# A two-layer trunk on one core: loads and squares at the start, fill ahead of two attention steps, one unit's sums and the last row block

## The chip, the cores and the metric

The kernel runs on one core of a Trainium2 chip. The time is device microseconds of one execution, and less is better. The profile's engines are PE (TensorE), DVE (VectorE), ACT (ScalarE), POOL (GpSimd) and SP (SyncE, which here issues nearly all DMAs).

## What is computed

Sixteen learned rows (meta) are put ahead of 512 input rows of width 1024. Then come one layer of gated linear attention (GLA) and one of differential softmax attention, each an RMSNorm, one wide input projection, the mixing, a gate and an output projection that is added to the rows. A last RMSNorm drops the meta rows.

```python
h = concatenate([meta, x])                       # 528 rows of 1024
for i in range(2):
    hn = rmsnorm(h, g_norm[i])                   # h * rsqrt(mean(h*h) + eps) * g
    y = gla_branch(hn, ...) if i == 0 else diff_branch(hn, ...)
    h = h + y
return rmsnorm(h[16:], g_final)

# diff_branch: q, k, v, z = split(hn @ w_in); per head (8 heads, two maps of width 128):
#   s = q @ k.T / sqrt(128) + bias;  p = softmax(s);  a = p[0] - lam * p[1];  o = a @ v
#   o = o * rsqrt(mean(o*o) + eps) * gnorm * (1 - lambda_init)
#   y = (silu(z) * o) @ w_out
```

## The kernel before

**Arithmetic.** Every f32 operand of a large matmul is held as a high and a low part. ACT copies the high part (line 284), DVE subtracts it to get the low part (line 285), and PE multiplies in three passes. Plain projections run at line 430 with 512 columns. Most others are a `Unit`: a 2x2 block product made of seven smaller ones with 256 or 264 columns (line 440), whose weight sums DVE forms (`sums`, line 375). ACT copies a partial product of a unit out of its bank (`u`, line 461) before PE may add the next product on top of it, and DVE adds the outputs (lines 495 and 497).

**Order of the work.** PE's order is written by hand. Projections are generators in a queue, and a planner `W` deals them out: `W.fill(c)` issues products of about c microseconds of its own estimate and then the next attention step comes. If the queue is empty, a fill issues nothing. A head has 14 steps over four row blocks, taken from block 3 down to block 0: A is the scores and the exponentials, B transposes the softmax rows and splits them (`aT`, `am`), C multiplies by the values (lines 409 and 1773) and normalizes a row block, E transposes two finished blocks (line 1789), multiplies by the gate into `yt` and splits it into `hT`. The last three steps of a head are B(0), C(0) and E(0). C's chain is: ACT puts a constant beside the values (line 1777), squares and sums them (1778), POOL takes the power (1780), ACT scales (1781); line 1789 reads the result `on`. In the last head only the first six steps (A(3), A(2), B(3), A(1), C(3), B(2)) lie between units; the others alternate with the output projection by row block (`final_rows`, called F3 to F0 in that order, each in two parts; line 1863), whose weights ACT and DVE split into tiles called `x`. The orders on DVE, ACT and POOL are the scheduler's, from the program and its own costs, except at the start and in the last row block, where they follow the program text. Every engine takes its instructions in order. `W.mark` is the DVE addition that was issued last; `tc.issue_after(W.mark.ins)` keeps an instruction behind it in the order.

**Start.** SP loads the identity, meta, x in four blocks of 128 rows (`x0` to `x3`: tiles `qs`, `ks`, and the two called `v`), the norm weights, a small weight `glr` and then the large weights (`raw`). For each block ACT squares and sums the rows (line 712), DVE and POOL make the factor (lines 564 and 565), DVE scales the rows in two halves (line 722), and PE transposes them (line 742), four blocks to a bank; unscaled rows are transposed too (730). When the fourth block is in, ACT and DVE take the transposed, scaled rows out of the banks (lines 800 and 801), split them, and the first projection starts. PE runs matmuls of ones (line 656) while it has nothing else.

**End.** F0 adds the last row block's output projection to the rows in three column parts of 512, 256 and 256 (line 1857, DVE), ACT squares and sums each part (1858), DVE adds the three sums (1870, 1871), DVE forms the first half times the last norm's weights, `hg` (1872), POOL takes the power (1873), ACT scales `hg` (1882) while DVE scales the other half (1880), and each half goes out by a DMA (1883).

Of the kernel before, what the change touches and what calls it, by code (L numbers as in the profile page):

```python
# [217 lines left out]
def trunk(ctx, tc, x, meta, g_norm, gla_w_in, gla_w_gate_up, gla_b_gate, gla_gnorm, gla_w_out,  # L218
# [146 lines left out]
    def want_unit(w, c0, calm=False):  # L365
# [11 lines left out]
        def sums(raw):  # L377
            t = T(wp, [P, 2, 512], F32, "sum", bufs=1)
            add(in_rows(t[:, 1, :]), block(raw, 2), block(raw, 3))
# [282 lines left out]
    sp.dma_start(ident, c_ident)  # L662
    xt = []
    grows = T(gp, [16, P], F32, "vm0")
    z2 = T(gp, [P, 2, D], F32, "z")
    v2 = [T(gp, [P, 2, D], F32, f"v{i}") for i in range(2)]
    for b in range(5):
        t0, n = BLK[b]
        t = T(gp, [P, D], F32, ("qs", "ks")[b - 1]) if b in (1, 2) else {0: z2, 3: v2[0], 4: v2[1]}[b][:, 1, :]
        sp.dma_start(t[:n], meta if b == 0 else x[(b - 1) * P:b * P])  # L670
        xt.append(t)
        if b == 2:
            sp.dma_start(grows, g_norm.rearrange("l (k p) -> (l k) p", p=P))
# [32 lines left out]
    sums0 = T(gp, [P, 10], F32, "sums0")  # L706
    raws = {}

    def squares(b):
        sq = z2[:, 0, :]  # L710
        n = BLK[b][1]
        act.activation(sq[:n], xt[b][:n], AF.Square, accum_out=sums0[:n, b:b + 1])

    def factor(b):
        n = BLK[b][1]
        rstd_of(sums0[:n, 5 + b:6 + b], sums0[:n, b:b + 1], D, n)

    def scaled(b, halves=range(2)):
        n = BLK[b][1]
        for i in halves:  # L720
            o = yt[i][:, b - 1, :512] if b else xm0[:NM, i * 512:(i + 1) * 512]
            dve.tensor_scalar(o, xt[b][:n, i * 512:(i + 1) * 512], sums0[:n, 5 + b:6 + b], None, op0=ALU.mult)
# [31 lines left out]
    for k in range(KT):  # L754
        pe.transpose(pm[:, k, :], xm0[:NM, k * P:(k + 1) * P], ident[:NM, :NM])
    raw_copy(1, 0, dve)
# [10 lines left out]
    pe.transpose(pm0[:, KT * NM:KT * NM + 16], grows, ident[:16, :16])  # L767
    turned(2, range(4))
    warm_up(3)
    scaled(3)  # L770
    turned(3, range(4))
    squares(4)
    factor(4)
# [3 lines left out]
    dve.tensor_tensor(xm, pm, g_sb[:, 0, :].unsqueeze(2).to_broadcast([P, KT, NM]), op=ALU.mult)  # L777
    for c in (0, 32, 64):
        act.activation(glr[:, :, c:c + RANK], glr_raw, AF.Copy)
    dve.tensor_tensor(glr[:, :, 96:], glr_raw, glr[:, :, :RANK].bitcast(F32), op=ALU.subtract)  # L780
    raw_copy(2, 0, act)
    raw_copy(2, 1, act)
    warm_up(3)
    scaled(4)
# [18 lines left out]
    scaled_pair(0)  # L803
    for k0 in range(0, KT, 2):
# [1039 lines left out]
    def final_rows(b, wt, yp):  # L1844
# [10 lines left out]
        def finish(i, cs):  # L1855
            hc = hacc[:, b, cs]
            dve.tensor_tensor(hc, hc, ps[i], op=ALU.add)
            act.activation(o[:, cs], hc, AF.Square, scale=1.0 if b else float(D) ** -0.5, accum_out=st[:, i:i + 1])
# [167 lines left out]
```

## Time and profile before

| | |
|---|---|
| median of three runs | 969.67 us (969.65, 969.67, 970.43) |
| profiled execution, its own time | 971.08 us |
| its span on the core | 968.4 us |
| mean granted clock of PE | 0.996 |
| busy: PE, DVE, ACT, POOL | 953.0, 798.2, 635.6, 81.3 us |
| moved by DMA | 104.96 MB, 108 GB/s over the span |

The timeline's rows give the start in microseconds from the span's start, the duration, engine, line, operation, output and inputs, and in brackets how long the engine sat idle before it and what released it. A row with "xN" joins N instructions. The rows of the waits give total, number and longest wait of one line for another. In the table by stage, a row gives the busy time of each engine in a stretch, with the number of instructions, then the granted clock of PE, the busy share of the DMA engines, and GB/s.

### The profile page before, as it was taken

The page shows a single profiled execution, that of the slowest core. Times are in us where ns is not written, and L with a number is a line of the kernel's source. Part 1 is how long each engine was busy: PE and PEld are TensorE (multiplying, and loading weights), DVE is VectorE, ACT ScalarE, POOL GpSimd, SP SyncE. Part 2 cuts the span into 40 slices and gives each one's busy share as a digit, 9 for nine tenths or more (in the row PEclk, how much of TensorE's full clock was granted, in tenths as well). Part 3 has the DMA queues.
Part 4 walks back from the last instruction along what each step waited for, and adds up shares of the span by engine and source line. Part 5 has one row for each costly group of instructions (what it writes and reads, how often), then busy time and mean ns, then how long its engine had stood idle before and what let it go on. Part 6 is the DMA issues. An engine that isn't in the chain of part 4 may idle for free.

```text
span 968.4 us, 18488 instructions
## 1 busy us (share of the span) xinstructions
PE 953.0 (98%) x7173; PEld 912.4 (94%) x7173; DVE 798.2 (82%) x1557; ACT 635.6 (66%) x1313; POOL 81.3 (8%) x164
## 2 busy tenths in 40 slices
PE   9999999999999999999999999999999999999997
PEld 8999999999999999998899898999999999989986
DVE  7989886886878787667997887879879889888875
ACT  7776755477647567656757685576766766755673
POOL 1000000000000000000001121111101101110111
PEclk9999999999999999999999999999999999999999
DMA  8322223635462237134356515234252261533312
GB/s 197 88 79 61 86 72 126 142 109 119 123 164 89 87 112 162 47 107 152 99 133 152 127 56 142 83 123 113 87 149 87 80 159 44 145 91 98 110 44 87
DMA packets 128602, 104.96 MB, mean 108 GB/s; under 512 B 51181, under 2 KB 112909, under 8 KB 128512
## 3 DMA queue, kind: packets, MB, share of 16 engines
q1 hardware_dynamic: 123184, 93.80, 35.3%
q10 hardware_dynamic: 5328, 9.95, 2.8%
q8 instruction: 57, 0.93, 0.4%
q14 instruction: 33, 0.27, 0.1%
HBM read 83.64 MB, written 11.80 MB: 99 GB/s over the span
## 4 chain that ended last, share of the span: by engine, by line
PE 73%; DVE 8%; ACT 4%; DMA 3%; issue 2%; POOL 1%; SPq 0%; POOLq 0%; DVEq 0%; ACTq 0%
PE bx L440 17%; PE bv L440 10%; PE by L440 9%; PE ps L409 7%; PE bx L997 5%; PE bx L430 4%; PE bx L409 3%; DMA raw<-in_diff_w_in_dram 3%; PE bv L997 2%; PE by L997 2%; PE ps L1239 2%; PE bv L409 1%; PE by L409 1%; DVE wl L285 1%; PE ps L1863 1%
## 5 line engine op out<-in xcount | busy, mean ns | idle before, releaser
L285 DVE TENSOR_TENSOR wl<-raw,wh 128x1024 fp32r<-128x1024 f32 x93 | 113.5, 1221 | 20.5 <-ACT wh L284 20.0
L284 ACT ACTIVATE wh<-raw 128x1024 fp32r<-128x1024 f32 x93 | 97.9, 1053 | 45.2 <-PE by L997 23.2
L440 PE MATMUL bv<-x,wh 128*128 128x264 f32 (+1 forms) x736 | 108.9, 285 | 0.1
L440 PE MATMUL bx<-x,wh 128*128 128x264 f32 (+1 forms) x720 | 105.6, 285 | 0.4 <-ACT ps L1777 0.4
L440 PEld LDWEIGHTS bv<-x,wh 128*128 128x128 f32 x736 | 96.8, 188 | 0.9 <-DVE z L497 0.3
L440 PEld LDWEIGHTS bx<-x,wh 128*128 128x128 f32 x720 | 94.4, 188 | 1.1 <-ACT ps L1777 0.7
L285 DVE TENSOR_TENSOR wl<-sum,wh 128x1024 fp32r<-128x1024 f32 x46 | 56.2, 1221 | 11.6 <-ACT wh L284 11.2
L461 ACT ACTIVATE u<-bx 128x264 f32<-128x264 f32 (+1 forms) x128 | 48.4, 378 | 21.8 <-PE bx L440 18.9
L440 PE MATMUL bv<-x,wl 128*128 128x264 f32 (+1 forms) x368 | 62.2, 286 | 0.1
L1735 ACT ACTIVATE p<-p,st 128x528 f32<-128x528 f32 (+3 forms) x64 | 36.4, 569 | 38.7 <-DVE st L1733 38.5
L440 PE MATMUL bx<-x,wl 128*128 128x264 f32 (+1 forms) x360 | 59.2, 284 | 0.0
L284 ACT ACTIVATE wh<-sum 128x1024 fp32r<-128x1024 f32 x46 | 48.4, 1051 | 10.4 <-PE bv L440 6.3
L440 PE MATMUL by<-x,a12h 128*128 128x264 f32 (+1 forms) x360 | 52.6, 285 | 0.9 <-DVE t L495 0.9
L440 PE MATMUL bx<-x,a11h 128*128 128x264 f32 (+1 forms) x360 | 53.0, 285 | 0.0
L440 PEld LDWEIGHTS bv<-x,wl 128*128 128x128 f32 x368 | 51.4, 188 | 0.4 <-issue 0.3
L284 ACT ACTIVATE a11h<-raw 128x512 fp32r<-128x512 f32 x46 | 28.9, 627 | 33.3 <-DMA raw<-in_diff_w_in_dram 12.8
L440 PEld LDWEIGHTS bx<-x,wl 128*128 128x128 f32 x360 | 50.0, 188 | 0.6 <-DVE wl L285 0.4
L440 PEld LDWEIGHTS bx<-x,a11h 128*128 128x128 f32 x360 | 47.8, 189 | 0.6
L440 PEld LDWEIGHTS by<-x,a12h 128*128 128x128 f32 x360 | 46.9, 188 | 1.1 <-DVE t L495 1.1
L565 POOL TENSOR_TENSOR st<-st,mhalf 128x1 f32<-128x1 f32 (+1 forms) x20 | 12.1, 606 | 386.5 <-DVE st L564 386.5
L1738 POOL TENSOR_TENSOR st<-st,minus 128x1 f32<-128x1 f32 x32 | 21.1, 658 | 279.4 <-ACT p L1735 226.4
L440 PE MATMUL by<-x,a22h 128*128 128x264 f32 (+1 forms) x280 | 40.1, 284 | 0.0
(501 smaller groups left out, 2671.8 us busy)
## 6 DMA issues: line engine op xcount, KB each, us to landing
raw<-in_diff_w_in_dram SPq DMA_DIRECT2D x52, 512.0 KB, 5.0
raw<-in_gla_w_in_dram SPq DMA_DIRECT2D x48, 512.0 KB, 4.5
raw<-in_gla_w_out_dram SPq DMA_DIRECT2D x8, 1024.0 KB, 6.0
raw<-in_diff_w_out_dram SPq DMA_DIRECT2D x8, 1024.0 KB, 5.3
raw<-in_diff_w_in_dram SPq DMA_DIRECT2D x6, 1024.0 KB, 6.0
vd<-planes ACTq DMA_DIRECT2D x12, 268.0 KB, 4.3
vd<-keep ACTq DMA_DIRECT2D x12, 264.0 KB, 2.3
T<-bdr SPq DMA_DIRECT2D x8, 264.0 KB, 3.8
```

What stands on the lines that cost most here:

```text
L284: act.activation(hi, src, AF.Copy)
L285: dve.tensor_tensor(lo, src, hi.bitcast(F32), op=ALU.subtract)
L409: pe.matmul(ps, l, r, start=first and n == 0, stop=last and n == 2, **kw)
L430: pe.matmul(bank, a[:, k, :], b[k] if n0 is None else b[k][:, n0 + i * nn:n0 + (i + 1) * nn], start=n == 0 and ks[0] == 0, stop=n == len(t ...
L440: pe.matmul(bank[:, :x[q].shape[2]], w[p][:, k * P:(k + 1) * P], x[q][:, k, :], start=first and i == 0, stop=i == len(PASSES) - 1, skip_gr ...
L461: W.moved = act.activation(t, self.bx[:, :self.n], AF.Copy, scale=self.sc)
L565: pool.tensor_tensor(dst, dst, mhalf[:np_, :dst.shape[1]], op=ALU.pow)
L997: pe.matmul(banks[i][:, :HT], h.t[p][:, k, mm * P:(mm + 1) * P], s.y[q][k][:, i * HT:(i + 1) * HT], start=n == 0, stop=n == len(PASSES) - 1)
L1239: pe.matmul(o, s.kd[:, i, kc], s.qs[:, i, t0:t0 + n], start=i == 0, stop=i == 1)
L1735: act.activation(p[:, :nk], p[:, :nk], AF.Exp, scale=-1.0, bias=st[:, m:m + 1], accum_out=st[:, 2 + m:3 + m])
L1738: pool.tensor_tensor(st[:, 5:6], st[:, 3:4], minus, op=ALU.pow)
L1863: pe.matmul(ps[i], yp[hd][p][:, k, b * P:(b + 1) * P], wt[q][cs.start // 512][:, 2 * hd + k, cs.start % 512:(cs.stop - 1) % 512 + 1], star ...
```

## The change

It has five places.

1. **Start.** Identity, meta and norm weights are issued from ACT's queue, ahead of its table load; SP issues the four blocks of x first. The last block's squares are divided: 512 columns on ACT, 512 on DVE, which adds them to a second accumulator; the factor is made from both (a DVE operation with the two as operands, then the power on POOL). The last block's first half is scaled on ACT, its second on DVE. The norm weights' transpose and what DVE makes of it stand earlier, one bank copy goes from ACT to DVE, the subtraction for `glr` stands behind the first rows of line 801, and the third group of warm-up matmuls is two instead of three. In the order that results on DVE, three small operations on constants (lines 1096, 1130, 1122) stand ahead of the casts of line 1046 instead of among the two operations of line 1051.
2. **Head 0, after B(0) (step 11 of 0 to 13):** the fill ahead of C(0) is 5.2 instead of 2.4.
3. **Last head, ahead of step 3, the scores A(1):** a fill of 1.3 is added where there was none.
4. **One unit** (the input projection's columns from 768, the queries of head 3): the first of the three weight sums is kept behind the addition that was issued last.
5. **F0:** the third part's squares go from ACT to DVE, chained with the two other sums in one operation; `hg` is made on POOL right behind the first addition; the second half is scaled and stored as two parts of 256.

```diff
@@ -376,7 +376,8 @@
 
         def sums(raw):
             t = T(wp, [P, 2, 512], F32, "sum", bufs=1)
-            add(in_rows(t[:, 1, :]), block(raw, 2), block(raw, 3))
+            with tc.issue_after(W.mark.ins) if (w is d_w_in and c0 in (768,)) else ExitStack():
+                add(in_rows(t[:, 1, :]), block(raw, 2), block(raw, 3))
             add(in_rows(t[:, 0, :]), in_rows(t[:, 1, :]), block(raw, 0))
             add(block(raw, 2), block(raw, 2), block(raw, 0))
             return t
@@ -659,18 +660,15 @@
 
 
     ident = cp.tile([P, P], F32, name="ident")
-    sp.dma_start(ident, c_ident)
-    xt = []
-    grows = T(gp, [16, P], F32, "vm0")
     z2 = T(gp, [P, 2, D], F32, "z")
     v2 = [T(gp, [P, 2, D], F32, f"v{i}") for i in range(2)]
-    for b in range(5):
-        t0, n = BLK[b]
-        t = T(gp, [P, D], F32, ("qs", "ks")[b - 1]) if b in (1, 2) else {0: z2, 3: v2[0], 4: v2[1]}[b][:, 1, :]
-        sp.dma_start(t[:n], meta if b == 0 else x[(b - 1) * P:b * P])
-        xt.append(t)
-        if b == 2:
-            sp.dma_start(grows, g_norm.rearrange("l (k p) -> (l k) p", p=P))
+    grows = T(gp, [16, P], F32, "vm0")
+    xt = [z2[:, 1, :], T(gp, [P, D], F32, "qs"), T(gp, [P, D], F32, "ks"), v2[0][:, 1, :], v2[1][:, 1, :]]
+    act.dma_start(ident, c_ident)
+    act.dma_start(xt[0][:NM], meta)
+    act.dma_start(grows, g_norm.rearrange("l (k p) -> (l k) p", p=P))
+    for b in range(1, 5):
+        sp.dma_start(xt[b], x[(b - 1) * P:b * P])
     glr_raw = T(gp, [P, KT, RANK], F32, "a0")
     sp.dma_start(glr_raw, g_w_in[:, 6144:6160].rearrange("(k p) c -> p k c", p=P))
 
@@ -703,23 +701,35 @@
 
     yt = [T(gp, [P, 4, L], F32, f"y{i}") for i in range(2)]
     xm0 = v2[0][:, 0, :]
-    sums0 = T(gp, [P, 10], F32, "sums0")
+    sums0 = T(gp, [P, 11], F32, "sums0")
     raws = {}
 
-    def squares(b):
+    def squares(b, e=D):
         sq = z2[:, 0, :]
         n = BLK[b][1]
-        act.activation(sq[:n], xt[b][:n], AF.Square, accum_out=sums0[:n, b:b + 1])
-
-    def factor(b):
+        act.activation(sq[:n, :e], xt[b][:n, :e], AF.Square, accum_out=sums0[:n, b:b + 1])
+        if e < D:
+            dve.tensor_tensor_reduce(sq[:n, e:], xt[b][:n, e:], xt[b][:n, e:], op0=ALU.mult, op1=ALU.add, scale=1.0,
+                                     scalar=D * EPS, accum_out=sums0[:n, 10:11])
+
+    def factor(b, e=D):
         n = BLK[b][1]
-        rstd_of(sums0[:n, 5 + b:6 + b], sums0[:n, b:b + 1], D, n)
-
-    def scaled(b, halves=range(2)):
+        o = sums0[:n, 5 + b:6 + b]
+        if e == D:
+            rstd_of(o, sums0[:n, b:b + 1], D, n)
+        else:
+            dve.tensor_scalar(o, sums0[:n, b:b + 1], sums0[:n, 10:11], 1.0 / D, op0=ALU.add, op1=ALU.mult)
+            pool.tensor_tensor(o, o, mhalf[:n, :1], op=ALU.pow)
+
+    def scaled(b, halves=range(2), eng=None):
         n = BLK[b][1]
         for i in halves:
             o = yt[i][:, b - 1, :512] if b else xm0[:NM, i * 512:(i + 1) * 512]
-            dve.tensor_scalar(o, xt[b][:n, i * 512:(i + 1) * 512], sums0[:n, 5 + b:6 + b], None, op0=ALU.mult)
+            src, f = xt[b][:n, i * 512:(i + 1) * 512], sums0[:n, 5 + b:6 + b]
+            if eng is act:
+                act.activation(o, src, AF.Copy, scale=f)
+            else:
+                dve.tensor_scalar(o, src, f, None, op0=ALU.mult)
 
     def raw_turn(b, halves=range(2)):
         n = BLK[b][1]
@@ -753,6 +763,7 @@
     pm = pm0[:, :KT * NM].rearrange("p (k m) -> p k m", k=KT)
     for k in range(KT):
         pe.transpose(pm[:, k, :], xm0[:NM, k * P:(k + 1) * P], ident[:NM, :NM])
+    pe.transpose(pm0[:, KT * NM:KT * NM + 16], grows, ident[:16, :16])
     raw_copy(1, 0, dve)
     squares(2)
     scaled(1)
@@ -764,24 +775,24 @@
     squares(3)
     scaled(2)
     factor(3)
-    pe.transpose(pm0[:, KT * NM:KT * NM + 16], grows, ident[:16, :16])
     turned(2, range(4))
-    warm_up(3)
-    scaled(3)
-    turned(3, range(4))
-    squares(4)
-    factor(4)
     g_sb = cp.tile([P, 2, KT], F32, name="g_sb")
     dve.tensor_copy(g_sb, pm0[:, KT * NM:KT * NM + 16].rearrange("p (l k) -> p l k", l=2))
     xm = tmp()[:, :KT * NM].rearrange("p (k m) -> p k m", k=KT)
     dve.tensor_tensor(xm, pm, g_sb[:, 0, :].unsqueeze(2).to_broadcast([P, KT, NM]), op=ALU.mult)
+    warm_up(2)
+    squares(4, 512)
+    scaled(3, [0])
+    factor(4, 512)
+    scaled(3, [1])
+    turned(3, range(4))
+    raw_copy(2, 0, act)
     for c in (0, 32, 64):
         act.activation(glr[:, :, c:c + RANK], glr_raw, AF.Copy)
-    dve.tensor_tensor(glr[:, :, 96:], glr_raw, glr[:, :, :RANK].bitcast(F32), op=ALU.subtract)
-    raw_copy(2, 0, act)
-    raw_copy(2, 1, act)
     warm_up(3)
-    scaled(4)
+    scaled(4, [0], act)
+    scaled(4, [1])
+    raw_copy(2, 1, dve)
     turned(4, range(4))
 
     b12 = x_parts(6)
@@ -801,6 +812,7 @@
         dve.tensor_scalar(xg[i][:, k0 % 4 + 1, NM:], pts[k0 + 1], g_sb[:, 0, k0 + 1:k0 + 2], None, op0=ALU.mult)
 
     scaled_pair(0)
+    dve.tensor_tensor(glr[:, :, 96:], glr_raw, glr[:, :, :RANK].bitcast(F32), op=ALU.subtract)
     for k0 in range(0, KT, 2):
         if k0 + 2 < KT:
             scaled_pair(k0 + 2)
@@ -1855,7 +1867,14 @@
         def finish(i, cs):
             hc = hacc[:, b, cs]
             dve.tensor_tensor(hc, hc, ps[i], op=ALU.add)
-            act.activation(o[:, cs], hc, AF.Square, scale=1.0 if b else float(D) ** -0.5, accum_out=st[:, i:i + 1])
+            if i < 2:
+                act.activation(o[:, cs], hc, AF.Square, scale=1.0 if b else float(D) ** -0.5, accum_out=st[:, i:i + 1])
+            else:
+                dve.scalar_tensor_tensor(st[:, 3:4], st[:, 0:1], EPS, st[:, 1:2], op0=ALU.add, op1=ALU.add)
+                dve.tensor_tensor_reduce(o[:, cs], hc, hc, op0=ALU.mult, op1=ALU.add, scale=1.0 / D, scalar=st[:, 3:4],
+                                         accum_out=st[:, 4:5])
+            if b == i == 0:
+                pool.tensor_tensor(hg, hc, gfin[:, cs], op=ALU.mult)
 
         def part(hd):
             for i, cs in enumerate(parts):
@@ -1867,15 +1886,11 @@
                     finish(i, cs)
             if hd:
                 if b == 0:
-                    dve.scalar_tensor_tensor(st[:, 3:4], st[:, 0:1], EPS, st[:, 1:2], op0=ALU.add, op1=ALU.add)
-                    dve.tensor_tensor(st[:, 4:5], st[:, 2:3], st[:, 3:4], op=ALU.add)
-                    dve.tensor_tensor(hg, hacc[:, b, :512], gfin[:, :512], op=ALU.mult)
                     pool.tensor_tensor(st[:, 4:5], st[:, 4:5], mhalf[:, :1], op=ALU.pow)
                 else:
                     dve.tensor_reduce(st[:, 3:4], st[:, 0:3], axis=AX.X, op=ALU.add)
                     rstd_of(st[:, 4:5], st[:, 3:4], D)
-                for i in range(2):
-                    cs = slice(512 * i, 512 * (i + 1))
+                for i, cs in enumerate(parts):
                     if b or i:
                         dve.scalar_tensor_tensor(o[:, cs], hacc[:, b, cs], st[:, 4:5], gfin[:, cs], op0=ALU.mult, op1=ALU.mult)
                     else:
@@ -1949,6 +1964,8 @@
                     W.finish(values[hd])
                 W.settle()
                 W.fill(2.0)
+            if last and n == 3:
+                W.fill(1.3)
             if n == 4:
                 W.land()
             if n == 5 and gates[hd] in W.queue:
@@ -1966,7 +1983,7 @@
                 if not last:
                     heads[hd + 1].T = bias_tile(hd + 1)
             W.fill(max((W.left - keep) * share[f] / sum(share[g] for g, _ in steps[n:]),
-                       ((4.0, 3.0, 5.2, 3.0, 4.6, 3.0, 4.0, 3.0)[hd]) if n == len(steps) - 2 else {A: 0.0, B: 2.4, C: 2.4, E: 1.0}[f]))
+                       ((4.0, 3.0, 5.2, 3.0, 4.6, 3.0, 4.0, 3.0)[hd]) if n == len(steps) - 2 else {A: 0.0, B: 2.4 if hd or n < 11 else 5.2, C: 2.4, E: 1.0}[f]))
     W.finish()
     W.settle()
     ws.pump()
```

At the end of head 0 the order on PE before, from the last eight products of the queries' projection (`wl`) to the transposes of step E and the next head's first product:

```order
L430 MATMUL bx_9632<-x_1512_8556,wl_9561 128x512 x4
L430 MATMUL bx_9632<-x_1514_8558,wl_9561 128x512 x4
L1789 MATMUL ps_9669<-ident,on_9647 128x128 [waits Activation_49]
L1789 MATMUL ps_9669<-ident,on_9596 128x128
L1789 MATMUL ps_9669<-ident,on_9647 128x128
L1789 MATMUL ps_9669<-ident,on_9596 128x128
L440 MATMUL bx_9692<-x_1512_8556,a11h_9688 128x256 [waits DVE_49,PE_49]
```

and with the change:

```order
L431 MATMUL bx_9632<-x_1512_8556,wl_9561 128x512 x3
L431 MATMUL bx_9632<-x_1514_8558,wl_9561 128x512 x4
L410 MATMUL ps_9657<-v_1525_8729,aT_1685_9618 128x256 [waits Activation_49]
L410 MATMUL ps_9657<-v_1526_8730,aT_1685_9618 128x256
L410 MATMUL ps_9657<-v_1525_8729,aT_1686_9619 128x256 [waits DVE_49]
L1785 MATMUL ps_9657<-vm_8731,am_9617 128x256 [waits DVE_49]
L1801 MATMUL ps_9669<-ident,on_9662 128x128 [waits Activation_49]
L1801 MATMUL ps_9669<-ident,on_9596 128x128
L1801 MATMUL ps_9669<-ident,on_9662 128x128
L1801 MATMUL ps_9669<-ident,on_9596 128x128
L441 MATMUL bx_9692<-x_1512_8556,a11h_9688 128x256 [waits DVE_49,PE_49]
```

The values of row block 0 (tiles `v` and `vm`) stood ahead of fifteen products, the last eight of which are the first two rows before; now they stand between the last of these and the transposes that read their normalized result `on`.

On ACT behind that place, before (`q` is the query copy, `u` the next unit's partial product, `v` and `planes` the next values' split, held back by `tick`, which DVE writes behind `yt`):

```order
L287 ACTIVATE q_1687_9628<-bx_9632 128x512 [waits PE_49]
L284 ACTIVATE a11h_9830<-raw_9685 128x512 [waits DMAHW7_49,PE_49]
L461 ACTIVATE u_9707<-bx_9692 128x256 [waits PE_49]
L284 ACTIVATE hT_8777<-yt_9674 128x2x256 [waits DVE_49]
L598 ACTIVATE v_1708_9734<-planes_9386,tick_9705 128x4x128 [waits DMAHW5_49,DMAHW4_49,DVE_49]
L598 ACTIVATE v_1708_9734<-planes_9386,tick_9705 128x4x128
```

and with the change:

```order
L287 ACTIVATE q_1687_9628<-bx_9632 128x512 [waits PE_49]
L1789 ACTIVATE ps_9657<-st_9415 128x1 [waits PE_49]
L1790 ACTIVATE on_9662,st_9415<-ps_9657 128x257 [waits Activation_49]
L1793 ACTIVATE on_9662<-ps_9657,st_9415 128x256 [waits Pool_49]
L284 ACTIVATE hT_8777<-yt_9674 128x2x256 [waits DVE_49]
L599 ACTIVATE v_1708_9734<-planes_9386,tick_9705 128x4x128 [waits DMAHW5_49,DMAHW4_49,DVE_49]
L462 ACTIVATE u_9707<-bx_9692 128x256 [waits PE_49]
L599 ACTIVATE v_1708_9734<-planes_9386,tick_9705 128x4x128
```

The partial product `u_9707` stood ahead of the split of `yt` and of the two value splits, and now stands behind the first and between the two others.

At the start the order on DVE before, from the last block's factor to the first two rows of line 801:

```order
L564 TENSOR_SCALAR sums_23_163<-sums_23_163 128x1 [waits Activation_49]
L775 COPY g_sb<-ps_184 128x16 [waits PE_49]
L777 TENSOR_TENSOR t_242<-ps_184,g_sb 128x128 [waits DVE_49]
L780 TENSOR_TENSOR kd_157<-a_16_131,kd_157 128x8x16 [waits DMAHW7_49,Activation_49]
L722 TENSOR_SCALAR y_21_161<-v_13_122,sums_23_163 128x512 [waits DMAHW6_49,Pool_49]
L722 TENSOR_SCALAR y_22_162<-v_13_122,sums_23_163 128x512
L801 TENSOR_SCALAR y_35_260<-bx_201,g_sb 128x512 [waits DVE_49,PE_49]
L801 TENSOR_SCALAR y_35_260<-by_203,g_sb 128x512
```

and with the change (ISA is the multiply-and-sum of half the last block):

```order
L712 ISA z_118,sums_23_163<-v_12_120 128x512 [waits DMAHW6_49]
L712 ISA sums_23_163 128x1
L732 TENSOR_SCALAR y_21_161<-v_11_119,sums_23_163 128x512 [waits DMAHW5_49,Pool_49]
L721 TENSOR_SCALAR sums_23_163<-sums_23_163 128x1 [waits DVE_49,Activation_49]
L732 TENSOR_SCALAR y_22_162<-v_11_119,sums_23_163 128x512
L732 TENSOR_SCALAR y_22_162<-v_12_120,sums_23_163 128x512 [waits Pool_49]
L748 COPY hT_90<-ps_214 128x4x128 [waits PE_49]
L812 TENSOR_SCALAR y_35_259<-bx_202,g_sb 128x512 [waits DVE_49,PE_49,Activation_49]
L815 TENSOR_TENSOR kd_157<-a_16_131,kd_157 128x8x16 [waits DMAHW7_49]
```

Half of the squares is new on DVE and stands ahead of the third block's scaling, whose two halves stand around the last block's factor; a scaling of 512 columns has left DVE, and a bank copy (748) has come to it.

## The prediction

> **What bounds the kernel now.** I read the page's busy shares first, then the waits of PE, then PE's busy time by stage.
>
> ```profile
> PE 953.0 (98%) x7173; PEld 912.4 (94%) x7173; DVE 798.2 (82%) x1557; ACT 635.6 (66%) x1313; POOL 81.3 (8%) x164
> ```
>
> ```profile
> PE ps L409 <- DVE vm L421: 1.1, 1, 1.1
> PE by L440 <- DVE t L495: 0.9, 1, 0.9
> PE bx L742 <- DVE y L722: 0.8, 1, 0.8
> ```
>
> ```profile
> 26.00:940.00 914.00, 907.77 (x6883) 871.76 (x6883) 762.26 (x1478) 603.85 (x1241) 73.20 (x146) 1.00 0.38 107
> 630.00:690.00 60.00, 60.00 (x457) 57.95 (x456) 52.05 (x105) 41.30 (x93) 7.76 (x16) 1.00 0.39 113
> ```
>
> PE's work sets the time: between 26 and 940 us it is idle for 914.00 - 907.77 = 6.23 us. The change takes no product away, so it can win only in such holes, at the start and at the end. The noise to beat is 0.2%, 1.94 us. The waits listed are single events; the change reaches those at L742 and L409 and leaves `by` L440 alone.
>
> **Start.** The last block of x is late, and a chain of one engine after another follows it.
>
> ```profile
> 11.06 1.06 ACT L712 ACTIVATE z<-v 128x1024 f32<-128x1024 f32 x1 [0.42 <-DMA v<-in_x_dram]
> 12.29 0.15 DVE L564 TENSOR_SCALAR sums<-sums 128x1 f32<-128x1 f32 x1
> 12.52 0.55 POOL L565 TENSOR_TENSOR sums<-sums,mhalf 128x1 f32<-128x1 f32 x1 [1.06 <-DVE g_sb L775]
> 13.10 0.88 DVE L722 TENSOR_SCALAR y<-v,sums 128x512 f32<-128x512 f32 x2
> 13.64 0.44 PE L742 MATMUL bx<-ident,y 128*128 128x128 f32 x2
> ```
>
> The squares (11.06 to 12.12), the factor (12.29), the power (12.52) and the scaling (13.10) lie end to end. Half of the squares takes about half of 1.06, 0.53, or 0.6 with ACT's fixed part; on DVE the other half runs beside it. That gives 0.45. The two scaled halves, 0.88 together on DVE, then run side by side, but PE waits only for the first half (0.54 from 13.10 to 13.64) at first; ACT takes about 0.6 for it, which loses 0.05. The block's own arrival stays: its DMA is issued earlier by the three issues that leave SP's queue, but in the seven us before it the DMA engines are full:
>
> ```profile
> 4.87:8.29 3.42, 2.32 (x22) 1.89 (x21) 2.29 (x6) 2.15 (x4) 1.05 (x2) 1.00 0.91 319
> 8.29:11.70 3.41, 3.41 (x16) 2.88 (x17) 1.58 (x6) 2.42 (x6) 1.10 (x2) 0.50 1.15 296
> ```
>
> (The last columns are the granted clock, the DMA engines' share and GB/s.) Nearly the same bytes come ahead of it, so I take 0.2 for it. I take 0.45 + 0.2 - 0.05 = 0.60. DVE now has a half of the third block's scaling (0.44) ahead of the factor; if that is in the way and the arrival doesn't move, 0 is left. If the arrival moves by more, with ACT's idle 0.42 ahead of the last squares gone too, it is 1.1.
>
> A second piece lies at 31 us.
>
> ```profile
> 30.43 0.17 DVE L1096 TENSOR_SCALAR gn_sb<-gn_sb 128x16 f32<-128x16 f32 x1
> 30.71 0.43 DVE L1051 TENSOR_TENSOR a<-bx,a 16x264 fp32r<-16x264 f32 x1
> 31.19 2.09 PE L903 MATMUL bx<-x,wh 128*128 128x264 f32 x15 [0.35 <-DVE a L1051]
> ```
>
> With the small operations out of the way, L1051 starts at 30.43 and PE waits 0.28 less; they move into idle time of DVE ahead of the casts. Start in all: -0.9 (0.6 + 0.3), between -0.3 and -1.4.
>
> **Head 0.**
>
> ```profile
> 541.89 1.22 DVE L285 TENSOR_TENSOR wl<-raw,wh 128x1024 fp32r<-128x1024 f32 x1
> 541.89 1.63 POOL L1780 TENSOR_TENSOR st<-st,mhalf 128x1 f32<-128x1 f32 x1 [8.88 <-ACT on L1778]
> 545.19 0.71 PE L409 MATMUL ps<-v,aT 128*128 128x256 f32 x3 [0.83 <-ACT aT L284]
> 545.92 0.39 PE L1773 MATMUL ps<-vm,am 96*128 96x256 f32 x1
> 546.15 1.80 PE L430 MATMUL bx<-x,wh 128*128 128x512 f32 x7
> 547.69 0.47 ACT L1781 ACTIVATE on<-ps,st 128x256 f32<-128x256 f32 x1 [0.66 <-POOL st L1780]
> 548.61 0.69 DVE L375 TENSOR_TENSOR sum<-raw 128x512 f32<-128x512 f32 x1 [0.89 <-DMA raw<-in_diff_w_in_dram]
> 549.65 0.60 PE L1789 MATMUL ps<-ident,on 128*128 128x128 f32 x4
> 551.77 0.37 ACT L461 ACTIVATE u<-bx 128x256 f32<-128x256 f32 x1
> 552.29 0.68 DVE L1792 TENSOR_TENSOR yt<-ps,z 128x512 f32<-128x512 f32 x1
> 552.92 1.10 PE L440 MATMUL bx<-x,wh 128*128 128x256 f32 x8
> 553.00 0.63 ACT L284 ACTIVATE hT<-yt 128x512 fp32r<-128x512 f32 x1 [0.86 <-DVE tick L639]
> 553.54 1.32 ACT L598 ACTIVATE v<-planes,tick 128x512 fp32r<-128x512 f32 x2
> ```
>
> POOL's power, held for 1.63 instead of 0.55, made `aT` late, and PE waited. Fifteen products of the queries follow, (549.65 - 546.15) / 15 = 0.233 each, and they cover the chain from the values to `on`. The longer fill puts all fifteen ahead of the values, and the projection is the last thing in the queue. So the old wait goes (products from 545.19 less 0.83 and the gap's own rest of 0.15, 544.21), but the cover goes too. The values start at 544.21 + 15 x 0.233 = 547.71, L1773 at 548.07. From L1773 to the end of L1781 it was 548.16 - 545.92 = 2.24, so the transposes come at 550.35 against 549.65: 0.70 later, after an idle PE of some 1.9.
>
> There is a second wait behind it. From the transposes to the product at 552.92 (`bx` on top of a bank that `u` has copied) it is 3.27, so PE would be there at 553.62. On ACT `u` now stands behind the split of `yt` and one value split. `yt` does not come earlier, since DVE's sums ahead of it wait for a DMA until 548.61, and from there DVE is busy to 552.29. So ACT starts `hT` at 553.00, the value split at 553.54, `u` half of 1.32 less 0.05 later, 554.15, and ends it at 554.53; PE goes on at 554.57, 1.65 later than before. From there on PE was busy without a hole, so 1.65 stays: I take +1.65. The lower bound is +0.70 (no wait for `u`). The upper is +2.3: a low clock in the stretch from 551 adds at most 0.6, since what it slows runs partly into the wait for `u`.
>
> The rows at the start show that clock at half speed (8.29 to 11.70) behind a stretch in which PE was busy for 2.32 with short matmuls, but it was full behind another stretch with as little work:
>
> ```profile
> 923.05:926.47 3.42, 2.23 (x16) 1.99 (x16) 3.28 (x8) 1.77 (x6) 0.41 (x1) 1.00 0.34 87
> 926.47:929.88 3.41, 3.41 (x31) 3.41 (x30) 2.41 (x6) 3.21 (x5) 1.06 (x3) 1.00 0.57 220
> ```
>
> **Last head.**
>
> ```profile
> 924.19 1.37 PE L409 MATMUL ps<-k,q 128*128 128x272 f32 x6 [1.11 <-DVE vm L421]
> 933.63 1.22 DVE L285 TENSOR_TENSOR x<-raw,x 128x1024 fp32r<-128x1024 f32 x1
> 938.35 0.43 DVE L285 TENSOR_TENSOR hT<-yt,hT 128x256 fp32r<-128x256 f32 x1 [0.26 <-ACT hT L284]
> 939.28 1.09 PE L1863 MATMUL bx<-x,hT 128*128 128x512 f32 x4
> ```
>
> Twelve products of 256 columns (8 take 1.10 - 0.16 = 0.94 from start to start, 0.118 each, so 1.42) now run in the hole of 1.11 and a little behind it, and the scores start nearly when they did: PE is up to 1.3 ahead. The next thing that is late is the split of the output weights, whose DMA lands as before, and behind it `hT`, which was ready at 938.78 for PE's 939.28, only 0.50 of slack. Its chain runs over ACT, which takes the scaling of the values first, and that waits for POOL's power; the power now comes at about 933.2, next to the DVE row of 933.63 moved ahead. If it is held as at 541.89 (1.63 - 0.55 = 1.08), the lead is gone but for a part of 0.50. I take -0.5 between -1.3 and 0.1.
>
> **One unit's sums.** In its stretch (630 to 690, row above) PE has no idle time before, and the DVE rows stand with idle time about them (52.05 of 60). A sum that is later by one addition still comes ahead of its reader. 0, within 0.2.
>
> **Last row block.**
>
> ```profile
> 961.93 0.42 ACT L1858 ACTIVATE x<-keep 128x256 f32<-128x256 f32 x1
> 962.55 0.69 DVE L1872 TENSOR_TENSOR t<-keep,x 128x512 f32<-128x512 f32 x1
> 962.77 0.87 POOL L1873 TENSOR_TENSOR fst<-fst,mhalf 128x1 f32<-128x1 f32 x1 [4.51 <-DVE fst L1871]
> 963.68 0.75 DVE L1880 SCALAR_TENSOR_TENSOR x<-keep,fst,x 128x512 f32<-128x512 f32 x1 [0.44 <-POOL fst L1873]
> ```
>
> Before, the power came due at 962.63, when the sums were added, and ended at 963.64, 0.4 behind L1872 on DVE. After, the third part is there at 961.9 (ACT read it at 961.93), the sum of the two others takes 0.15, the multiply-and-sum some 0.5 from 962.05 by ACT's row, the power 0.55 (line 565's row) from 962.65, and DVE's two parts of 0.42 end at 964.1 in place of 964.43: -0.4. `hg` on POOL has no row of its size. The nearest are DVE's 0.69 and POOL's copy of 64 columns in 0.24:
>
> ```profile
> 14.37 0.24 POOL L799 COPY y<-t 128x64 f32<-128x64 f32 x1 [1.30 <-PE by L742]
> ```
>
> Eight of these are 1.92, so it ends between 961.5 and 962.75; I take the middle, 962.1, which meets the multiply-and-sum for 0.05. At 962.75 it holds the power and, if a two-input DVE operation can't run beside it, the sum too: then the end is 0.3 later than before, not 0.4 earlier. [...]
>
> **Sum.** -0.9 + 1.65 - 0.5 + 0 - 0.4 = -0.15 us. The profiled execution took 971.08 with a span of 968.4, so 2.7 lie around the span; the median is 969.67, 1.4 under that execution, and I set the sum against the median: 969.5.
>
> **Rivals.** *Faster: head 0 costs only its first wait and the last head's hole closes.* If `u` isn't behind (DVE reaches `yt` earlier, or later holes such as `by` L440's 0.9 take the lag up) and POOL's power is free at 933.2: -0.9 + 0.70 - 1.3 - 0.4 = -1.9, or -2.4 with the start's 1.4: 967.5. For it: PE is alone on the critical path there. Against it: ACT's order is fixed, and `hT` had only 0.50. 0.25.
>
> *Slower: POOL's power at head 0 starves.* It comes due near 549.1, where DVE's sums (L375) and a split run one upon the other from 548.61 to 551.77, each with two inputs. At 541.89 the power got its turn behind one operation; if it gets it only behind the last, it ends at 552.2, the transposes come at 552.7, PE idles 4.2 and `u` is behind it again: 552.7 + 3.27 = 555.97, +3.05, and a clock at half for 3.41 adds up to 1.7. Sum -0.15 - 1.65 + 3.05 + 1.7 = +2.95: 972.6. It decides from the second operation that the power is held past. 0.15, with other losses of such a size at the start's clock.
>
> *The change does not do what it says at the end:* `hg` ends late and the tail gives 0.3 instead of -0.4: +0.55, 970.2. 0.12; the price of the copy speaks for it.
>
> **How the numbers follow.** Forecast 0.48, the late `hg` 0.12, faster 0.25, slower 0.15. Forecast and late `hg` are within 0.2%, though a small part of either lies beyond: faster 0.28, same 0.57, slower 0.15. The forecast's own range is 968.2 to 970.9: 1.3 or so to each side, about half of what the terms' bounds add up to (-2.7 with every lower one, +2.6 with every upper one). For 8 in 10 it reaches to the faster case and most of the way to the slower: 967.0 to 971.9.
>
> **What would show it.** Right: no wait for `aT` at 545 but one of about 1.9 for `on` at the transposes and one near 1 for `u` behind it; no wait for `vm` at 924, while F3's second part starts within 0.5 of its old distance from there; the first scaled rows out of the banks (line 800, now 811) at 13.7; the last DMA's issue 0.4 sooner behind the last addition. Wrong: PE without a hole between 545 and 556, or a granted clock under 1.00 there; an F3 that keeps the whole lead of 1.3.

## The result

The changed kernel is slower: 976.0 us median of six runs (975.11 to 976.66) against 970.1 us (969.65 to 972.02) for the kernel before. The ratio is 1.0059, with a 95% interval of 1.0049 to 1.007. Forecast were 969.5 us, and a range that ended at 971.9. The profiled execution took 975.97 with a span of 973.8, which is 5.4 us longer than the span before.

PE's busy time grew by 2.8 us, 1.8 of it in the last head and behind it, where the granted clock was 0.56 for a stretch, and its largest waits are others now. From the page's busy shares and PE's waits with the change:

```profile
PE 955.8 (98%) x7171; PEld 915.1 (94%) x7171; DVE 798.6 (82%) x1560; ACT 635.3 (65%) x1311; POOL 85.3 (9%) x165
```

```profile
PE ps L1801 <- ACT on L1793: 2.2, 1, 2.2
PE ps L410 <- DVE yt L1804: 1.7, 1, 1.7
...
PE bv L441 <- DVE t L496: 1.0, 1, 1.0
PE by L441 <- DVE t L496: 0.8, 1, 0.8
```

The waits at 545 (`aT`) and 924 (`vm`) are gone, as the change meant, and three others of 2.2, 1.7 and 1.0 us have come. To see where the time went, the same matmul's start is compared in the two profiled executions (start after less start before):

| place, in the time of before | later than before, us | step |
|---|---|---|
| last block's first transpose, 13.64 | +1.20 | start |
| 31.19, behind the small DVE operations | +0.88 | start, 0.32 given back |
| 396.87 | +1.04 | start in all, after a new hole of 0.3 at 38 |
| transposes of E(0) of head 0, 549.65 | +2.01 | head 0, +0.97 |
| product behind `u`, 552.92 | +2.31 | head 0, +0.30 more |
| 702.83 | +2.50 | |
| 766.74 | +3.72 | a new wait, +1.2 |
| 829.15 | +3.95 | |
| bv L440 behind the scores A(1), 932.29 | +2.43 | last head, 1.5 ahead |
| values of C(2), 938.01 | +4.52 | last head, lead lost |
| 942.82 | +6.05 | last head, low clock |
| end of the span, 968.4 | +5.4 | end, -0.65 |

**The start after.** These rows of the timeline answer to those of before (meta's squares were at 3.42, the last block's power at 12.52, its first transpose at 13.64):

```profile
5.54 1.06 ACT L710 ACTIVATE z<-z 16x1024 f32<-16x1024 f32 x1 [2.04 <-DMA z<-in_meta_dram]
6.73 1.06 ACT L710 ACTIVATE z<-qs 128x1024 f32<-128x1024 f32 x1
...
10.61 0.63 ACT L710 ACTIVATE z<-v 128x512 f32<-128x512 f32 x1
...
12.02 0.68 DVE L712 CUSTOM_DVE_ANT_0 z<-v 128x512 f32<-128x512 f32 x1
...
13.02 0.21 DVE L721 TENSOR_SCALAR sums<-sums 128x1 f32<-128x1 f32 x1
...
13.31 0.72 POOL L722 TENSOR_TENSOR sums<-sums,mhalf 128x1 f32<-128x1 f32 x1 [0.98 <-DVE sums L721]
...
14.84 0.44 PE L752 MATMUL bx<-ident,y 128*128 128x128 f32 x2
```

Meta, 16 rows, lands 2.1 us later than before, and ACT, which squares it first, waits for it with x0 there already (PE took `qs` at 5.58). From there each block's chain is late. The last block is there at 10.61 (ACT takes it then), 0.45 earlier than before, but DVE comes to its half of the squares only at 12.02, behind the scaling of the block two before it and the constants.

**Head 0 after:**

```profile
549.18 0.28 PE L1785 MATMUL ps<-vm,am 96*128 96x256 f32 x1
549.27 0.69 DVE L375 TENSOR_TENSOR sum<-raw 128x512 f32<-128x512 f32 x1 [0.72 <-DVE q L288]
...
550.00 0.69 DVE L375 TENSOR_TENSOR sum<-sum,raw 128x512 f32<-128x512 f32 x1
...
550.27 0.83 POOL L1792 TENSOR_TENSOR st<-st,mhalf 128x1 f32<-128x1 f32 x1 [5.94 <-ACT on L1790]
...
551.13 0.47 ACT L1793 ACTIVATE on<-ps,st 128x256 f32<-128x256 f32 x1 [0.94 <-POOL st L1792]
...
551.66 0.66 PE L1801 MATMUL ps<-ident,on 128*128 128x128 f32 x4 [2.20 <-ACT on L1793]
...
553.66 0.63 ACT L284 ACTIVATE hT<-yt 128x512 fp32r<-128x512 f32 x1 [2.06 <-DVE tick L640]
554.20 0.71 ACT L599 ACTIVATE v<-planes,tick 128x512 fp32r<-128x512 f32 x1
...
554.81 0.36 ACT L462 ACTIVATE u<-bx 128x256 f32<-128x256 f32 x1
...
555.23 1.21 PE L441 MATMUL bx<-x,wh 128*128 128x256 f32 x8
```

PE stands idle for 2.20 us at the transposes, and nothing covers the chain from the values to `on`.

**The last head after:**

```profile
936.78 1.22 DVE L285 TENSOR_TENSOR x<-raw,x 128x1024 fp32r<-128x1024 f32 x1
936.78 1.62 POOL L1792 TENSOR_TENSOR st<-st,mhalf 128x1 f32<-128x1 f32 x1 [3.32 <-ACT on L1790]
...
938.44 0.47 ACT L1793 ACTIVATE on<-ps,st 128x256 f32<-128x256 f32 x1 [1.74 <-POOL st L1792]
...
941.96 0.42 DVE L1804 TENSOR_TENSOR yt<-ps,z 128x256 f32<-128x256 f32 x1
...
942.53 2.26 PE L410 MATMUL ps<-y,aT 128*128 128x256 f32 x9 [1.69 <-DVE yt L1804]
```

POOL's power starts with DVE's last split of the output weights and takes 1.62. ACT waits for it in its order, and with ACT the second gate (`z`) and `yt`. The values of C(2) need `yt` gone before them, and PE waits 1.69. Its clock is at half speed behind that: the stretches' table, with PE's busy time, the granted clock and the DMA columns at the end,

```profile
938.70:942.10 3.40, 1.92 (x12) 1.35 (x10) 1.68 (x4) 2.36 (x6) 0.00 (x0) 1.00 0.00 0
942.10:945.50 3.40, 2.97 (x12) 2.91 (x13) 1.52 (x7) 1.75 (x7) 0.94 (x3) 0.56 0.02 5
```

**The end after:** `hg` takes 1.28 on POOL, done at 968.16, and the power is due at 968.7, so it holds up nothing. From the last addition's start (967.53) to the power's end it is 1.87 instead of 2.16, and the last part's DMA is smaller.

```profile
966.88 1.28 POOL L1877 TENSOR_TENSOR t<-keep,x 128x512 f32<-128x512 f32 x1 [2.57 <-DVE keep L1869]
...
968.21 0.49 DVE L1874 CUSTOM_DVE_ANT_0 x<-keep,fst 128x256 f32<-128x256 f32 x1
...
968.85 0.55 POOL L1889 TENSOR_TENSOR fst<-fst,mhalf 128x1 f32<-128x1 f32 x1 [0.69 <-DVE fst L1874]
```

### The profile page after: what moved, and what is told of

The parts are those of the page before. It is cut to its first block, busy times and chain, and to the rows that moved or that the text cites. A ratio compares the mean times of both kernels' runs of the same rounds, so it can differ in the third digit from the quotient of the medians.

```text
span 973.8 us, 18482 instructions
## 1 busy us (share of the span) xinstructions
PE 955.8 (98%) x7171; PEld 915.1 (94%) x7171; DVE 798.6 (82%) x1560; ACT 635.3 (65%) x1311; POOL 85.3 (9%) x165
## 4 chain that ended last, share of the span: by engine, by line
PE 65%; DVE 11%; DMA 5%; ACT 5%; issue 2%; POOL 1%; SPq 0%; DVEq 0%; POOLq 0%; ACTq 0%
PE bx L441 15%; PE bv L441 9%; PE by L441 8%; PE ps L410 6%; PE bx L1009 5%; DMA raw<-in_diff_w_in_dram 4%; PE bx L431 3%; PE bx L410 3%; PE by L1009 2%; PE bv L1009 2%; DVE wl L285 2%; PE ps L1251 2%; DVE sum L375 2%; PE bv L410 1%; PE by L410 1%
## 5 line engine op out<-in xcount | busy, mean ns | idle before, releaser
L375 DVE TENSOR_TENSOR sum<-raw 128x512 f32<-128x512 f32 x46 | 31.7, 688 | 10.5 <-DMA raw<-in_gla_w_in_dram 5.0
```

The costliest lines, as they stand in the source:

```text
L375: dve.tensor_tensor(o, a, b, op=ALU.add)
```

## The experiments

Ratios are to the kernel before in the same runs, with 95% intervals.

### One part at a time

Each of these four is the kernel before with one part of the diff shown above, whole: the start, the fill of 5.2, the fill of 1.3, and the kept-back sums with the last row block.

> The start's edits alone (loads from two queues, x first, divided squares, the third block scaled around the factor). Theory, from the trace of the whole change: the first transposes of the last block come at 14.8 us instead of 13.6, of the 1.2 us 0.1 or so is given back by 38 us, and nothing later changes: about 1.1 us slower than before, 971.0. Rival, the prediction's term: the start by itself is 0.9 us faster, 969.0, and the loss seen in the whole change comes from a clock or a DMA that the other edits disturb.

Measured: 972.51 us, ratio 1.0031 (1.002 to 1.0043). The first transpose of the last block came at 14.87, 1.2 later, as in the whole change. The trace was still 1.2 behind at 707; the rest of its 2.2 came at 767 and 774, in steps of 0.4 to 0.5 each. The prediction's gain isn't there, and the start alone loses 2.7 us in the median, more than the 1.1 expected.

> Only the longer fill ahead of C(0) in head 0. Theory: the wait for aT (0.83 us at 545) goes, a wait of 2.1 to 2.2 us for on appears at the transposes, and PE passes the product behind u 1.2 us later than before: 971.1. Rival, the prediction's term: u is behind by 1.0 more, since here yt isn't moved by a late start: 1.65 us later, 971.5. A gain of 0.5 us or more would say that the hole at 545 was closed for good.

Measured: 972.64 us, ratio 1.0025 (1.0015 to 1.0036), single runs from 971.06 to 974.63. The wait for `aT` is gone and that for `on` is 2.2, as expected; the transposes are 1.67 behind those of before, of which 0.8 came ahead of head 0, so 0.9. Then PE ran at half clock:

```profile
548.00:551.40 3.40, 1.20 (x8) 0.88 (x7) 2.69 (x5) 1.61 (x5) 0.83 (x1) 0.97 0.06 17
551.40:554.80 3.40, 3.40 (x17) 3.40 (x18) 2.71 (x6) 1.24 (x2) 0.00 (x0) 0.52 0.44 122
554.80:558.20 3.40, 3.40 (x31) 3.40 (x31) 2.19 (x5) 3.21 (x7) 0.00 (x0) 1.00 0.56 194
```

PE was busy for 1.20 of 3.40 us in the first stretch, and in the next it did 17 matmuls, where it did 31 at full clock in the one after; by its end it was 3.24 behind, 1.57 more than at the transposes. In that execution `u` was there before PE, so the clock took the place of the wait that the prediction had priced. In the profile of the whole change the same gap (1.20 of 3.40 us busy from 548.5 on) was followed by a full clock:

```profile
548.50:551.90 3.40, 1.20 (x9) 0.90 (x8) 2.64 (x5) 1.61 (x5) 0.83 (x1) 1.00 0.03 8
551.90:555.30 3.40, 3.34 (x29) 3.13 (x27) 2.71 (x6) 1.64 (x4) 0.00 (x0) 1.00 0.47 125
```

So the same gap had two prices; what sets the two executions apart was not shown.

> Only the fill ahead of A(1) in the last head. Theory: the wait of 1.1 us at 924 goes, POOL's power of C(3) starts beside the DVE row that splits the output weights and is held to about 1.6 us, and PE waits 1.0 to 1.7 us for yt at the values of C(2); with a half clock behind it the kernel is 0.7 to 2.0 us slower, 970.6 to 971.7; without the half clock 0 to 0.7 slower. Rival, the prediction's term: 0.5 us faster, 969.3.

Measured: 970.81 us, ratio 1.0014 (1.0002 to 1.0026), single runs from 969.43 to 973.8. The power was held (932.00, 1.63 beside DVE's 1.22), the wait for `yt` was 1.69, and PE, which was 2.2 us ahead at 932 (0.8 of that from ahead of the last head's fill), was 0.3 ahead at the values of C(2), then 1.3 behind after a stretch at a clock of 0.59. The theory holds; the forecast gain of 0.5 doesn't.

> The kept-back sums of the one unit and the last row block together; they lie 300 us apart, so the trace tells them apart. Theory: sums 0, tail 0.65 us faster, as in the whole change: 969.2. Rival: the sums are behind the wait of 1.0 us for t near 770 us that the whole change shows and the kernel before doesn't; then that wait is here too, and the time is 970.3 to 970.6.

Measured: 968.95 us, ratio 0.9991 (0.9981 to 1.0). There is no wait near 766 or 770, where the whole change has one, so the kept-back sums aren't behind that. From the last matmul (960.44) to the end it is 6.56 instead of 7.24: the end gains 0.68.

The medians of these four lie 2.74, 2.87 and 1.04 us over and 0.82 under the kernel before, 5.83 together, and the whole change lies 5.9 over. Each is good to about 1 us, and within that the parts add up, so nothing here asks for a loss that needs two parts at once.

### The start: whose fault

```diff
     act.dma_start(ident, c_ident)
-    act.dma_start(xt[0][:NM], meta)
     act.dma_start(grows, ...)
+    sp.dma_start(xt[0][:NM], meta)
     for b in range(1, 5):
         sp.dma_start(xt[b], x[(b - 1) * P:b * P])
```

The first kernel has these loads and the squares, factors and order of the kernel before; the second has these loads and all the rest of the changed start.

> The loads of the change (identity and norm weights on ACT's queue, x on SP's), but meta first on SP's queue, and the arithmetic of the start as before. Theory: what cost the start most is meta landing at 5.5 us instead of 3.4, because it shared the DMA engines with x from the other queue; first in its own queue it lands by 3.6, the last block of x by 10.7, and the last block's first transpose comes at 13.0 to 13.4 us against 13.64 before: 0.3 to 0.6 faster, 969.3. Rival: loads from two queues slow each other whatever their order, and that transpose comes at 13.9 or later.

Measured: 968.58 us, ratio 0.9989 (0.998 to 0.9999). Meta is there at 3.16, and the last block's first transpose comes at 12.78, 0.86 earlier than before:

```profile
3.16 1.06 ACT L709 ACTIVATE z<-z 16x1024 f32<-16x1024 f32 x1
...
10.07 1.06 ACT L709 ACTIVATE z<-v 128x1024 f32<-128x1024 f32 x1 [0.42 <-DMA v<-in_x_dram]
...
12.78 0.44 PE L739 MATMUL bx<-ident,y 128*128 128x128 f32 x2 [0.28 <-DVE y L719]
```

That is more than expected. Two queues are no loss; meta's late landing was. Meta goes to SP's queue and to the head of it in one step here, so the runs don't tell these two apart.

> The whole start of the change, with meta first on SP's queue. If meta's landing is the cause of all of the loss, the last block's first transpose comes at 13.2 us or before (14.84 in the whole change), and the time is 0.4 to 0.8 under the kernel before: 969.1. If the divided squares cost by themselves, since DVE does them in its order behind the other blocks' work, it comes at 13.9 to 14.5, and the time is 0.2 to 0.9 above: 970.3. The second takes the part of the loss that e5 doesn't explain.

Measured: 969.91 us, ratio 1.0002 (0.9993 to 1.0012). The transpose comes at 13.25, 0.39 before the old time and 0.47 behind the kernel with undivided squares:

```profile
10.14 0.63 ACT L709 ACTIVATE z<-v 128x512 f32<-128x512 f32 x1 [0.39 <-DMA v<-in_x_dram]
...
10.43 0.68 DVE L711 CUSTOM_DVE_ANT_0 z<-v 128x512 f32<-128x512 f32 x1
...
11.44 0.20 DVE L720 TENSOR_SCALAR sums<-sums 128x1 f32<-128x1 f32 x1
11.56 0.47 DVE L731 TENSOR_SCALAR y<-v,sums 128x512 f32<-128x512 f32 x1
...
11.72 0.72 POOL L721 TENSOR_TENSOR sums<-sums,mhalf 128x1 f32<-128x1 f32 x1 [0.99 <-DVE sums L720]
12.47 0.72 ACT L729 ACTIVATE y<-v,sums 128x512 f32<-128x512 f32 x1 [0.54 <-POOL sums L721]
```

The transpose lies between the two expectations. With meta first the start gains, so meta's landing costs 14.84 - 13.25 = 1.6. But the rest of the changed start, the divided squares with what goes with them, costs 0.47. (The gain isn't in the time: in this profile PE is 0.4 ahead until 766 and 0.7 behind from there, by the wait that is left open below.) Undivided, ACT's squares begin at 10.07 and the factor's DVE operation at 11.42; divided, ACT begins at 10.14, DVE ends its half at 11.1, and the factor comes at 11.44, since a half of the third block's scaling stands ahead of it. The power then takes 0.72 instead of 0.55, and ACT takes 0.72 for the first half's scaling, where DVE's first half let PE go on 0.55 after it began. Nothing was won in the squares, and three steps behind them got longer.

### Head 0: share the cover

```diff
-  ... {A: 0.0, B: 2.4, C: 2.4, E: 1.0}[f]
+  ... {A: 0.0, B: 2.4 if hd or n < 11 else 3.4, C: 2.4, E: 1.0}[f]
```

> Head 0, fill of 3.4 in place of 2.4 or 5.2: six more products go ahead of the values and nine stay behind them. Theory: the two waits are for two chains, and fifteen products of 0.233 us cover both if they are shared out: six take 1.4 us, more than the hole of 1.0 (start to start), and nine take 2.1 against the 2.24 of the chain from the values to on. Then no wait over 0.4 us is left between 540 and 556, the transposes come 0.8 to 1.1 us earlier and the time is 968.8. Rival: aT and on are late for the same reason (POOL's power held by DVE), the wait comes back in full at one of the two places, and the time is the same as before.

Measured: 969.38 us, ratio 0.9999 (0.9989 to 1.0008), single runs from 968.51 to 972.02. Neither wait is left in head 0: the values start at 545.69 with no wait before them, the transposes at 548.41 instead of 549.65,

```profile
545.69 0.51 PE L409 MATMUL ps<-v,aT 128*128 128x256 f32 x3
...
547.12 0.55 POOL L1780 TENSOR_TENSOR st<-st,mhalf 128x1 f32<-128x1 f32 x1 [4.03 <-ACT on L1778]
547.89 0.47 ACT L1781 ACTIVATE on<-ps,st 128x256 f32<-128x256 f32 x1
548.41 0.66 PE L1789 MATMUL ps<-ident,on 128*128 128x128 f32 x4
```

1.24 earlier, though PE was 0.1 behind when it came to head 0's end. The place gains 1.3, more than was expected. In the profiled execution it was given away elsewhere: 0.9 in small steps up to 922, and then the old wait of 1.1 us at 924 was followed by half clock,

```profile
921.50:924.90 3.40, 2.15 (x13) 1.47 (x13) 3.26 (x8) 2.37 (x7) 0.00 (x0) 0.98 0.14 7
924.90:928.30 3.40, 3.40 (x18) 3.40 (x18) 1.47 (x6) 1.48 (x3) 0.55 (x1) 0.52 0.79 301
```

which cost 1.5. In the profile of the kernel before, the clock behind that wait was full (1.00 from 926.47 to 929.88). The interval of the ratio holds no gain and a gain of 1.0 alike; whether the lead is kept is seen in the last two kernels.

### The last head: a shorter hold

```diff
-            split(*[t[j][i][:, :, c:c + 256] for j in range(2)], raw[:, :, c:c + 256])
+            o = [t[j][i][:, :, c:c + 256] for j in range(2)]
+            if i == 0 or c == 0:
+                split(*o, raw[:, :, c:c + 256])
+            else:
+                act.activation(o[0], raw[:, :, c:c + 256], AF.Copy)
+                for k in (0, 2):
+                    dve.tensor_tensor(o[1][:, k:k + 2], raw[:, k:k + 2, c:c + 256], o[0][:, k:k + 2]..., op=ALU.subtract)
```

> The last head's fill of 1.3, with DVE's last split of the output weights (1024 columns, 1.22 us) done as two of 512 (0.6 each). Theory: POOL's power of C(3) is held for the length of one DVE operation; it then takes 0.55 to 1.1 us instead of 1.62, yt and the values of C(2) come 0.5 to 1.0 us earlier than with the fill alone, PE's wait for yt falls from 1.7 to 0.7 to 1.2, and the time is 0.4 to 1.0 under the fill alone: 969.9. Rival: the power isn't what makes yt late (the raw weights' landing is); then the wait stays at 1.6 or more and the time is the same as with the fill alone, 970.8.

Measured: 969.39 us, ratio 0.9997 (0.9988 to 1.0007), single runs from 968.79 to 969.78.

```profile
932.34 0.68 DVE L1817 TENSOR_TENSOR x<-raw,x 128x512 fp32r<-128x512 f32 x1
932.34 1.09 POOL L1780 TENSOR_TENSOR st<-st,mhalf 128x1 f32<-128x1 f32 x1 [3.25 <-ACT on L1778]
...
936.69 0.56 PE L409 MATMUL ps<-k,q 128*128 128x144 f32 x3 [1.05 <-DVE am L419]
```

The DVE operation is 0.54 shorter and the power too (1.63 to 1.09): it is held for the length of that operation, 0.41 past its end in both. The wait for `yt` is gone; one of 1.05 for `am` has come in its place, since ACT's `am` copies stand behind the gate's. The lead isn't kept, but nothing is lost any more, and the time is 1.4 us under that of the fill alone.

### What is worth keeping

The first kernel has the loads with meta first, undivided squares, the fill of 3.4 and the last row block of the change. The second adds the fill of 1.3 with the halved split.

> The parts that proved to gain, alone: the loads with meta first, undivided squares, the fill of 3.4 in head 0, the last row block of the change; no fill ahead of A(1) in the last head and no kept-back sums. If the gains add: 1.1 (loads) + 1.0 (head 0) + 0.65 (end), 2.7 us under the kernel before, 967.0. If the clock at half speed behind the wait of 1.1 us at 924, which came in one execution of the fill of 3.4, eats part of them: 967.5 to 968.5.

> The same with the last head's fill of 1.3 and the halved split of the output weights. In its own run that pair moved a wait of 1.1 us from 924 to 937 and won nothing on the path. Theory: no gain again, within 0.4 us of the kernel without it; but its spread is smaller, since no single stretch of idle PE is over 1.1 us. Rival: with PE earlier by 2 us the weights' landing is later in comparison, PE waits for the split itself, and it is 0.5 to 1.0 slower than the kernel without it.

Measured: 967.37 us, ratio 0.9977 (0.9967 to 0.9986), and 967.38 us, ratio 0.9976 (0.9967 to 0.9985). The gains add: 2.44 us against 1.13 + 0.82 + 0.33 = 2.28 of the three kernels with one of the parts (meta first, the last row block, the fill of 3.4), each good to about 1 us. The lead of head 0 is kept: the first kernel is 1.31 ahead of the kernel before at 540, 2.65 at the transposes, and 2.5 or more from there to the last matmul. The last head's fill is worth nothing in the medians. In the profiles its kernel, 1.28 behind the first one at 921 (no run shows why), comes to the transposes of `on` at 933.57, 0.39 ahead of the first one's 933.96, then waits 0.98 for `am`, and the values of C(2) start at 935.77 against 935.09: 1.1 of the 1.7 won is lost again. Its runs spread no less (966.22 to 969.43 against 966.83 to 968.56). So the first, simpler one is the better version; it beats both kernels, by 2.4 and about 8.5 us.

## Why the prediction was wrong

**What bounds the kernel** was right: products weren't touched, and the 5.4 us lie in PE's holes, the start, the end and a stretch of low clock.

**Start: -0.9 forecast, +1.0 measured at 397 us** (and 2.7 in the median of the start alone). This step failed, and with the wrong sign; what it named as a sign, the first scaled rows out of the banks at 13.7, came at 15.59. It asked when the last block lands and what of its chain is shortened. "Nearly the same bytes come ahead of it" was right for the last block (it was ready 0.45 earlier). But the first load in the chain, meta, was moved behind 512 KB of another queue, and I priced no later arrival for it. Every block's squares stand behind meta's on ACT. With meta first the same two queues are 0.86 ahead. The second half of the step failed too: divided squares were to win 0.45 and cost 0.47; its bound of 0, with a half of the third block's scaling in the way, named that row and stopped too early. The 0.28 at 31 us came as forecast (0.32) and was given back at 38, where DVE, still 1.2 behind, was what PE waited for.

**Head 0: +1.65 forecast, +1.3 measured** in the whole change's profile (2.4 with half clock in that of the fill alone, whose median is 2.9 over), in the direction and by the chain that the step described: cover gone, idle PE of 2.2 (1.9 forecast), the transposes 0.97 later (0.70; POOL's power was held for 0.83), and a wait for `u`, of 0.3 instead of 1.0. ACT's chain was as the step said (`u` 1.15 behind `hT`, 553.66 to 554.81); but PE itself came 0.27 later than forecast, and `hT` was only 0.66 later than before, while the start had put PE 1.04 behind: DVE's sums ahead of `yt` began at 549.27 instead of 548.61. The bound for the clock, 0.6, was too small: it fell to 0.52 for 3.4 us in one execution, and head 0 came to 2.4 there against an upper bound of 2.3.

**Last head: -0.5 forecast, +2.1 measured.** The mechanism was in the text: the power held beside the moved DVE row by 1.08 (1.07 measured), so that the lead is gone. The step then stopped at `hT` and F3. It didn't ask who else waits for the late gate: `yt` comes ahead of the values of C(2), 1.3 us before F3's second part, and behind the wait stood half clock (0.56). Both terms, 1.69 and some 1.5, were missing, and the upper bound of 0.1 was wrong.

**Sums: 0**, as measured. **End: -0.4 forecast** (964.1 in place of 964.43 is -0.33), **-0.65 measured**; `hg` took 1.28, near the middle of 0.69 and 1.92 that was taken, and the rival with a late `hg` fell; its condition, that DVE's operation can't run beside `hg`, no run shows, since `hg` was done (968.16) before that operation began (968.21).

**The rivals.** The slower one named POOL's power starving at head 0; it was held past one operation only, so its point of decision wasn't reached, and the 976.0 measured lies beyond its 972.6 too, by other steps. The faster one fell with the held power and `yt`. The terms' lower bounds add up to -2.6, not -2.7, which changes nothing here.

**Open: the wait at 766, +1.2 us**, which the prediction has no term for. The whole change and the start with meta first have it (0.96 and 0.93), the start alone has 0.25, the others none; so it came only with the divided squares and what goes with them, in one profile of each. In these executions one of DVE's sums waits for a load of weights:

```profile
756.35 0.69 DVE L375 TENSOR_TENSOR sum<-raw 128x512 f32<-128x512 f32 x1 [1.68 <-DMA raw<-in_diff_w_in_dram]
```

The table of that load's DMA shows, in the last row of its queues, one packet of instructions on the same engines: 2.2% of an 8 us stretch in the whole change,

```profile
q8 instruction: 1, 0.02, 2.2%
```

2.2% again in the other one with the wait, 1.0% in the one with 0.25, and 0.7% in three that have none; where it is long, the load's last 2 us run at 20 to 26 GB/s, against 333 to 379 at its fullest. That is an association in six profiles. No experiment moved such a packet, so the cause of the wait, and why it falls there in some kernels, stay open.

## What to carry to other kernels

Before a load goes to another queue, list what else uses the DMA engines then, and ask first for the small load at the head of the chain: 64 KB behind 512 KB of another queue was 2 us late. Work that covers a wait is seldom free to move; here fifteen products covered two chains, and sharing them 6 to 9 closed both holes, where all in one place opened a larger. A gap of PE of 1.1 to 2.2 us, as here, should be priced with and without a stretch at half clock, 1.5 us or so each time, and a chain is followed to all who wait for each of its rows, bank and buffer releases too, not to the first that one thought of.

## What was not expected of the hardware

A matmul gap of 2.2 us cost no clock in one execution (granted clock 1.00) and a half-speed stretch of 3.4 us (0.52) in another of nearly the same code; gaps of 1.7 and 1.1 us were followed by one as well (0.56 and 0.52), the gap of 1.1 in the kernel with the fill of 3.4 and not in the kernel before (1.00). And a POOL operation on 128 single elements, 0.55 us alone, took 0.83, 1.09 and 1.62 beside DVE operations of two SBUF inputs that ran at its start, and ended 0.4 behind them each time. Where POOL came first (932.90 in the kernel before, DVE's gate product 0.13 later) neither was held: POOL took 0.55 and DVE 0.68.
